# Moving rows of the big products at one place against the weights: padded input slots and SwiGLU tiles, rows 384 apart

## The chip, the cores and the metric

One core of one Trainium2 chip. The metric is the device time of one execution in microseconds. The kernel is one launch; everything below happens on that core: TensorE multiplies, VectorE, ScalarE and GpSimd work elementwise, and DMA queues issued from SyncE, ScalarE and GpSimd bring data between HBM and SBUF.

## The reference

One inference step of a hybrid trunk with two layers, on 128 context tokens and 256 latent tokens of width 1024 in float32. Each layer is a half-step SwiGLU block, a mixer with four head groups (mLSTM, global attention, windowed attention, Hyena convolution) that share an input and an output projection, and a second SwiGLU block. Before each stands an RMSNorm whose shift, scale and gate come from a conditioning vector.

```python
def swiglu(h, wg, wu, wd):
    return (jax.nn.silu(h @ wg) * (h @ wu)) @ wd

def trunk_layer(x, mod, p, mixer):
    h = rmsnorm(x, p['g_ff1']) * (1 + part(1)) + part(0)
    x = x + 0.5 * part(2) * swiglu(h, p['w1_gate'], p['w1_up'], p['w1_down'])
    h = rmsnorm(x, p['g_mix']) * (1 + part(4)) + part(3)
    y, ctx_state = mixer(h)
    x = x + part(5) * y
    h = rmsnorm(x, p['g_ff2']) * (1 + part(7)) + part(6)
    x = x + 0.5 * part(8) * swiglu(h, p['w2_gate'], p['w2_up'], p['w2_down'])
```

The hidden width of SwiGLU is 2816, the joint input projection has 2832 columns, the modulation `silu(c) @ w_ada + b_ada` has 9 x 1024 columns per layer.

## The kernel before

All 384 tokens are worked on together, with the model width on the partitions: `x` is eight blocks of 128 partitions by 384 columns. A big product is done in three parts (`prod3`, L241 to L244): weights and rows are each split into a high half of type float32r and the low rest, and high x high (L242), high weights x low rows (L243) and low weights x high rows (L244) are added up in PSUM. Each part is one matmul with a 128x128 weight block as the stationary operand and a row of 384 columns as the moving one, preceded by its own weight load.

Weights come from HBM in tiles of 4096 bytes a partition (`weights_load`), are split by ScalarE and VectorE into the pools `whi` and `wlo` (`weights_split`, L237 and L238), and live there in four buffers each. Right behind those pools in SBUF lies the pool `hx` with four input slots `w0` to `w3`, taken by the functions `wide` (eight rows of 386 columns) and `flat` (the same bytes as a staging buffer for the modulation weights and the first input). The slots are allocated in the order of first use: 2, 3, 0, 1. A `Norm` holds its un-normed, gained input in one pair of slots (`alloc_x`: the high half `xh`, the low half `xl`, with two extra columns for the shift) and the normed input in the other pair (`alloc_h`: `hh` and `hl`). Layer 0's first block and layer 1's last block have their normed rows in slots 2 and 3, the two blocks between them in slots 0 and 1. `ch` and `cl` are the mixer's concatenated output, written into a pair of slots and read by the output projection.

A SwiGLU block (`ffn`) runs gate and up for eleven pairs of hidden columns, then down for four pairs of output columns. The first pair of columns uses the gained rows of 386 columns; all later ones the normed rows of 384. The hidden activations are kept split in 22 tiles `ah` and 22 tiles `al` of 384 columns (`hid_tiles`), allocated behind the pools `sm` (small tiles) and `ht` (scratch). Beside gate, up and down in the first three blocks runs the modulation of later sublayers: VectorE multiplies and adds `w_ada` rows (L272) from the slots that hold no rows.

In the mixer, q and k of the mLSTM are products like the above; the token-major products (`tok_major`, L759 to L761) take the rows as the stationary operand and stream 512 weight columns. `gsml` holds `g_mlstm` on all partitions: GpSimd issues its load at the mixer's start (L746), and VectorE multiplies the output gate `so` with it (L873). The tile `dg` of the pool `sm` (one buffer, 128 x 3 x 128) is written in `rbcast` (L425) and read by the product behind it (L427). In `hyena_filters`, `coarse` splits `filt_w1` into two tiles of the pool `filt`.

The instructions of an engine run in their queue's order. A planner of the tile framework places most of them by readiness; stretches under `manual_schedule` keep the written order. A tile's next user waits until its last reader has ended.

Of the kernel before, what the change touches and what calls it, by code (L numbers as in the profile page):

```python
# [9 lines left out]
F32 = mybir.dt.float32  # L10
F32R = mybir.dt.float32r
# [6 lines left out]
P = 128  # L18
DM = 1024
KD = DM // P  # L20
NP_, NS = 128, 256
NT = NP_ + NS
DEPTH = 2
# [67 lines left out]
def trunk_kernel(ctx: ExitStack, tc: tile.TileContext, I: dict, C: dict, O: list):  # L91
    nc = tc.nc
# [7 lines left out]
    hx = ctx.enter_context(tc.tile_pool(name="hx", bufs=1))  # L100
    sm = ctx.enter_context(tc.tile_pool(name="sm", bufs=2))
# [4 lines left out]
    def mm(name):  # L106
        return pmm.tile([P, 512], F32, tag="mm", name=name)

    def small(name):
        return psm.tile([P, 512], F32, tag="sm", name=name)  # L110
# [4 lines left out]
    def cload(name, shape, src, pool=None, eng=None):  # L115
        t = (pool or const).tile(shape, F32, name=name)
        (eng or nc.gpsimd).dma_start(out=t, in_=src)
        return t

    XC = NT + 2

    def wide(i):
        return hx.tile([P, KD, XC], F32R, tag=f"w{i}", name=f"wide{i}")

    def flat(i, n):
        return hx.tile([P, KD * XC], F32, tag=f"w{i}", name=f"flat{i}")[:, :n]

    rows, ctile = {}, {}  # L130

# [22 lines left out]

    cols_c = columns("c", [("c", row128(I["c"]), 8, nc.sync), ("c_ctx", I["c_ctx"].rearrange("(k p) -> k p", p=P), 8, nc.scalar)])
    xst = flat(2, 3 * DM).rearrange("p (b d) -> p b d", b=3)
    for b in range(3):
        nc.sync.dma_start(out=xst[:, b, :], in_=I["x_prompt"][0] if b == 0 else I["x_sample"][0, (b - 1) * P:b * P, :])
# [57 lines left out]
    def weights(src, nk, ncol, name, paired=False):  # L216
        return weights_split(weights_load(src, nk, ncol, name, paired), nk, ncol, name)
# [23 lines left out]
    def prod3(out, lh, ll, rh, rl, start, stop):  # L241
        T.matmul(out, lhsT=lh, rhs=rh, start=start, stop=False)  # L242
        T.matmul(out, lhsT=lh, rhs=rl, start=False, stop=False)  # L243
        T.matmul(out, lhsT=ll, rhs=rh, start=False, stop=stop)  # L244

    def split(src, hi, lo):
        S.copy(hi, src)  # L247
        V.tensor_tensor(out=lo, in0=src, in1=hi.bitcast(F32), op=ALU.subtract)
# [72 lines left out]
    def stager(pair):  # L321
        turn = [0]

        def stage(n):
            turn[0] ^= 1
            return flat(2 * pair + turn[0], KD * n * P).rearrange("p (k f) -> p k f", k=KD)
        return stage
# [49 lines left out]
    class Norm:  # L377
# [16 lines left out]
        def alloc_x(self):  # L394
            self.xh, self.xl = wide(2 * self.pair), wide(2 * self.pair + 1)
# [22 lines left out]
        def shift_cols(self):  # L418
            b = mod[:, self.l, self.sh * KD:(self.sh + 1) * KD, :]
            split(b, self.xh[:, :, NT:XC], self.xl[:, :, NT:XC])  # L420

# [7 lines left out]
            S.copy(self.r, rb[:, :NT])  # L429

        def alloc_h(self):
            th, tl = wide(2 - 2 * self.pair), wide(3 - 2 * self.pair)
            self.hh = [th[:, k, :NT] for k in range(KD)]
            self.hl = [tl[:, k, :NT] for k in range(KD)]

        def apply(self):
            self.alloc_h()
# [32 lines left out]
    def ffn(l, wg, wu, wd, gate, name, nm, nxt, units, mid=None, last=None, pre=None):  # L470
        with pre["pools"] if pre else ExitStack() as pools:
            ht = pre["ht"] if pre else pools.enter_context(tc.tile_pool(name="ht" + name, bufs=2, reuse_waits="tile"))
            ah, al = [], []

            def hid_tiles(i, f0, f1):
                hid = pools.enter_context(tc.tile_pool(name=f"hid{i}{name}", bufs=1, reuse_waits="tile"))
                for f in range(f0, f1):
                    for q, ts in (("h", ah), ("l", al)):
                        ts.append(hid.tile([P, NT], F32R, name=f"a{q}{f}"))
# [10 lines left out]
            def gate_up(j, kc):  # L490
                if (j, kc) not in ahead:
                    ahead[j, kc] = {q: weights(w_ap[l][kc * P:(kc + KC) * P, j * CW:(j + 1) * CW], KC, CW, f"{q}{name}{j}_{kc}")
                                    for q, w_ap in (("g", wg), ("u", wu))}
                return ahead[j, kc]
# [3 lines left out]
            def join(p, m):  # L498
# [3 lines left out]
                for i, q in enumerate("gu"):  # L502
                    S.copy(bt[:, i, :], p[q][m][:, NT:XC])
                joined[m] = sg, su, bt

            for j in range(KF // 2):
                early = j == 0
                first = early and pre
                p = pre if first else {"g": [mm(f"pg{m}") for m in range(2)], "u": [mm(f"pu{m}") for m in range(2)]}
                for kc in range(0, KD, KC) if not first else ():  # L510
                    w = gate_up(j, kc)
# [13 lines left out]
                    for i, (k, m, q) in enumerate(order):  # L525
                        kk = kc + k
                        lh, ll = w[q][0][:, k, m * P:(m + 1) * P], w[q][1][:, k, m * P:(m + 1) * P]
                        if early:
                            prod3(p[q][m][:, :XC], lh, ll, nm.xh[:, kk, :], nm.xl[:, kk, :], kk == 0, kk == KD - 1)
                        else:  # L530
# [19 lines left out]
                for m in range(2):  # L550
                    f = 2 * j + m
# [19 lines left out]
            for cp in range(4):  # L571
                pd = [mm(f"pd{m}") for m in range(2)]
                for k0 in range(0, KF, KC):
                    nk = min(KC, KF - k0)
                    w = weights(wd[l][k0 * P:(k0 + nk) * P, cp * CW:(cp + 1) * CW], nk, CW, f"d{name}{cp}_{k0}")
# [27 lines left out]
    def hyena_filters(fp):  # L603
# [4 lines left out]
        w1 = fp.tile([34, DEPTH, 64], F32, name="fw1")  # L608
# [33 lines left out]
        cols_f(tc.keep_in_program_order)  # L642
        fr = col("filt_freq")

        def coarse(t, shape, magic, name):
            c = fp.tile(shape, F32, name=name + "c")
            f = fp.tile(shape, F32, name=name + "f")
            tc.keep_in_program_order(V.tensor_scalar(out=c, in0=t, scalar1=magic, scalar2=None, op0=ALU.add))
            V.tensor_scalar(out=c, in0=c, scalar1=magic, scalar2=None, op0=ALU.subtract)
            V.tensor_tensor(out=f, in0=t, in1=c, op=ALU.subtract)  # L650
            return c, f

        w1c, w1f = coarse(w1, [34, DEPTH, 64], 1.5 * 2.0 ** 16, "fw1")
        frc, frf = coarse(fr, [P, 1], 1.5 * 2.0 ** 17, "ffr")
        pA, pB = small("fpsA"), small("fpsB")
        for l in range(DEPTH):
# [78 lines left out]
    def mixer(l, K, nm, nxt, fill):  # L737
# [4 lines left out]
        mes = ExitStack()  # L742
        ml = mes.enter_context(tc.tile_pool(name=f"ml{l}", bufs=1, reuse_waits="tile"))
        nm.shift_cols()
        gsml = ml.tile([P, 256], F32, name="gsml")
        nc.gpsimd.dma_start(out=gsml, in_=I["g_mlstm"][l:l + 1].partition_broadcast(P).rearrange("p o d -> p (o d)"))  # L746
        cmask = cload(f"cmask{l}", [P, 512], C["cmask"], mx)
        rope = cload(f"rope{l}", [P, 2, 2, HD], C["rope"].rearrange("(b p) a d -> p b a d", p=P), mx)

        def tok_major(ps, c0, name):  # L750
            for kc in range(0, KD, 2):
                w = weights(win_l[kc * P:(kc + 2) * P, c0:c0 + 512], 2, 512, f"{name}{kc}")
                fill(6)
                fill.flush(99)
                for b in range(3):
                    tb = slice(b * P, (b + 1) * P)
                    for k in range(2):
                        kk = kc + k
                        T.matmul(ps[b], lhsT=hh[kk][:, tb], rhs=w[0][:, k, :], start=(kk == 0), stop=False)  # L759
                        T.matmul(ps[b], lhsT=hl[kk][:, tb], rhs=w[0][:, k, :], start=False, stop=False)  # L760
                        T.matmul(ps[b], lhsT=hh[kk][:, tb], rhs=w[1][:, k, :], start=False, stop=(kk == KD - 1))  # L761
# [20 lines left out]
        for i, c0 in enumerate((C_AQ, C_AK)):  # L782
            p = [mm(f"pqk{m}") for m in range(2)]
            for kc in range(0, KD, KC):
                w = weights(win_l[kc * P:(kc + KC) * P, c0:c0 + CW], KC, CW, f"aqk{l}{i}{kc}")
                if i == 0 and kc:
                    rr = nm.rstd()
                for k in range(KC) if kc and i == 0 else (None,):
                    for m in range(2):
                        for k_ in (range(KC) if k is None else (k,)):  # L790
                            kk = kc + k_
                            prod3(p[m][:, :XC], w[0][:, k_, m * P:(m + 1) * P], w[1][:, k_, m * P:(m + 1) * P], nm.xh[:, kk, :], nm.xl[:, kk, :], kk == 0, kk == KD - 1)
                if i == 0 and kc:
                    nm.rbcast(rr)
                    nm.apply()
            pq += p
        hh, hl = nm.hh, nm.hl
        ch, cl = (wide(2 * nm.pair + i)[:, :, :NT] for i in range(2))

        def qk_scaled():  # L800
            for i in range(4):
# [59 lines left out]
                S.copy(gt[:, i, :, d * 4:d * 4 + 4], prv[:, i, :, d * GB:d * GB + 4])  # L861
        at, emt, wi = gt[:, 0], gt[:, 1], gt[:, 2, 1:3]

        pvo = [mm(f"pvo{b}") for b in range(3)]
        tok_major(pvo, C_AV, f"avo{l}")
        va = ml.tile([P, 3, 4, HD + 1], F32, name="va")
# [11 lines left out]
        for d in range(2):  # L878
            for par in range(2):
# [3 lines left out]
                                    in_=I["state_mlstm_n"][0, l, d].rearrange("(hh par) (d o) -> par d hh o", par=2, o=1)[par],  # L883
# [27 lines left out]
        for h in range(4):  # L911
            c = h // 2
# [418 lines left out]
        with tc.manual_schedule(engines={nc.tensor.engine}):  # L1331
# [4 lines left out]
            for q in range(2):  # L1336
                p = [mm(f"pwo{m}") for m in range(4)]
                for i, k0 in enumerate((0, 2, 4, 6)):
                    w_src = I["w_out"][l][k0 * P:(k0 + 2) * P, q * 512:(q + 1) * 512]
                    w = weights(w_src, 2, 512, f"wo{l}{q}{k0}", paired=k0 in (2, 4))  # L1340
# [23 lines left out]
    def start(sp):  # L1364
# [86 lines left out]
        load_ada(1, 1)  # L1451
        load_ada(0, 1)
        residual_in(n0.acc, flat(3, 3 * DM).rearrange("p (b d) -> p b d", b=3))
        for s in range(2):
            S.copy(sc32[:, :, s], sc[:, :, s])
# [56 lines left out]
    with tc.tile_pool(name="start", bufs=1, reuse_waits="tile") as sp, tc.manual_schedule():  # L1512
        start(sp)
    fps = ExitStack()
    filters = hyena_filters(fps.enter_context(tc.tile_pool(name="filt", bufs=1, side="right", reuse_waits="tile")))
    next(filters)

# [25 lines left out]
    nm = n0  # L1543
# [3 lines left out]
    for l in range(DEPTH):  # L1547
        nx = Norm(f"m{l}", l, 3, 4, pair=nm.pair)
        ffn(l, I["w1_gate"], I["w1_up"], I["w1_down"], 2, f"a{l}", nm, nx, plan["a", l], between if l == 0 else None, pre=p0 if l == 0 else None)
        nm, nx = nx, Norm(f"b{l}", l, 6, 7, pair=1 - nx.pair)  # L1550
        mixer(l, K, nm, nx, Filler(plan["m", l], small_stage))
        nm = nx
        nx = Norm("a1", 1, 0, 1, pair=nm.pair) if l == 0 else Norm("fin", early=False, pair=nm.pair)
        ffn(l, I["w2_gate"], I["w2_up"], I["w2_down"], 8, f"b{l}", nm, nx, plan["b", l])
        nm = nx
# [4 lines left out]
    for b in range(3):  # L1560
        y = wst.tile([P, WCH], F32, tag="wst", name=f"y{b}")
        for q in range(2):
            p = small("pfin")
# [37 lines left out]
```

## Time and profile before

| | us |
|---|---|
| three runs | 1649.02, 1646.46, 1649.88 |
| median | 1649.02 |
| the profiled execution | 1645.32 |
| its span, from first to last instruction | 1643.5 |
| TensorE busy in it | 1592.4 (97%) |
| VectorE busy | 1233.9 (75%) |
| ScalarE busy | 775.3 (47%) |

The profiled execution is one execution of the same program, recorded by the hardware profiler; its span lacks what lies ahead of the first and behind the last instruction. A busy share is an average over stages. Matmuls are pipelined: one begins before the last has drained, so their durations overlap, and the time that a product costs is the distance between two starts.

### The profile page before, as it was taken

The page shows a single profiled execution, that of the slowest core. Times are in us where ns is not written, and L with a number is a line of the kernel's source. Part 1 is how long each engine was busy: PE and PEld are TensorE (multiplying, and loading weights), DVE is VectorE, ACT ScalarE, POOL GpSimd, SP SyncE. Part 2 cuts the span into 40 slices and gives each one's busy share as a digit, 9 for nine tenths or more (in the row PEclk, how much of TensorE's full clock was granted, in tenths as well). Part 3 has the DMA queues.
Part 4 walks back from the last instruction along what each step waited for, and adds up shares of the span by engine and source line. Part 5 has one row for each costly group of instructions (what it writes and reads, how often), then busy time and mean ns, then how long its engine had stood idle before and what let it go on. Part 6 is the DMA issues. An engine that isn't in the chain of part 4 may idle for free.

```text
span 1643.5 us, 24971 instructions
## 1 busy us (share of the span) xinstructions
PE 1592.4 (97%) x9169; PEld 1497.7 (91%) x9169; DVE 1233.9 (75%) x2402; ACT 775.3 (47%) x1815; POOL 248.7 (15%) x334
## 2 busy tenths in 40 slices
PE   7899999999989999999999999999998999999997
PEld 4799999997867999999999999999776799999997
DVE  4899998996856699986999986697795567434333
ACT  4544444367454554443546444345835556333321
POOL 2122322241120001221220211113103000000000
PEclk9999999999999999999999999999999999999999
DMA  9667757853332367757667764765333234444341
GB/s 329 199 204 233 220 176 230 254 152 110 93 90 65 103 214 237 231 177 232 210 180 222 230 202 148 247 200 152 101 101 81 65 103 124 122 127 129 116 135 58
DMA packets 235855, 271.22 MB, mean 165 GB/s; under 512 B 14367, under 2 KB 220415, under 8 KB 235732
## 3 DMA queue, kind: packets, MB, share of 16 engines
q1 hardware_dynamic: 223232, 248.67, 49.0%
q0 software_dynamic: 9472, 20.30, 5.0%
q8 instruction: 72, 1.18, 0.3%
q10 hardware_dynamic: 3028, 0.64, 0.2%
q14 instruction: 51, 0.42, 0.1%
HBM read 257.62 MB, written 3.57 MB: 159 GB/s over the span
## 4 chain that ended last, share of the span: by engine, by line
PE 80%; DVE 12%; ACT 4%; issue 2%; DMA 1%; ACTq 0%; DVEq 0%
PE pg L242 7%; PE pg L243 7%; PE pg L244 7%; PE pu L244 7%; PE pu L243 7%; PE pu L242 7%; PE pd L244 5%; PE pd L243 5%; PE pd L242 5%; DVE adacc L272 4%; PE pwo L242 1%; PE pwo L243 1%; PE pwo L244 1%; PE pa L760 1%; PE pdu L242 1%
## 5 line engine op out<-in xcount | busy, mean ns | idle before, releaser
L272 DVE SCALAR_TENSOR_TENSOR adacc<-flat,sc,adacc 128x384 f32<-128x384 f32 (+1 forms) x602 | 353.5, 639 | 0.0
L296 POOL TENSOR_TENSOR adfold<-adacc,adfold 64x384 f32<-64x384 f32 (+1 forms) x86 | 119.5, 1390 | 138.3 <-DMA adfold<-adacc 135.8
L242 PE MATMUL pd<-ah,hi_da 128*128 128x384 f32 x352 | 120.1, 341 | 0.0
L244 PE MATMUL pd<-ah,lo_da 128*128 128x384 f32 x352 | 119.3, 339 | 0.8 <-DVE lo_da L238 0.8
L244 PE MATMUL pd<-ah,lo_db 128*128 128x384 f32 x352 | 119.3, 339 | 0.6 <-DVE lo_db L238 0.6
L243 PE MATMUL pg<-wide,hi_gb 128*128 128x384 f32 (+1 forms) x352 | 119.6, 340 | 0.2
L242 PE MATMUL pd<-ah,hi_db 128*128 128x384 f32 x352 | 119.7, 340 | 0.0
L242 PE MATMUL pg<-wide,hi_gb 128*128 128x384 f32 (+1 forms) x352 | 119.6, 341 | 0.0
L243 PE MATMUL pd<-al,hi_db 128*128 128x384 f32 x352 | 119.2, 339 | 0.0
L243 PE MATMUL pd<-al,hi_da 128*128 128x384 f32 x352 | 119.1, 338 | 0.0
L244 PE MATMUL pg<-wide,lo_gb 128*128 128x384 f32 (+1 forms) x352 | 119.0, 338 | 0.0
L243 PE MATMUL pu<-wide,hi_ub 128*128 128x384 f32 (+1 forms) x352 | 118.8, 338 | 0.0
L244 PE MATMUL pu<-wide,lo_ub 128*128 128x384 f32 (+1 forms) x352 | 118.4, 338 | 0.0
L242 PE MATMUL pu<-wide,hi_ub 128*128 128x384 f32 (+1 forms) x352 | 118.2, 337 | 0.0
L247 ACT CAST ah<-sg 128x384 fp32r<-128x384 f32 x88 | 45.0, 512 | 151.3 <-DVE sg L561 149.7
L292 POOL DMA_DIRECT2D adfold<-adacc x43 | 23.3, 542 | 599.1 <-DVE adacc L272 356.1
L242 PE MATMUL pg<-wide,hi_ga 128*128 128x384 f32 (+1 forms) x328 | 112.4, 343 | 0.0
L244 PE MATMUL pg<-wide,lo_ga 128*128 128x384 f32 (+1 forms) x328 | 111.2, 339 | 0.0
L243 PE MATMUL pg<-wide,hi_ga 128*128 128x384 f32 (+1 forms) x328 | 111.1, 339 | 0.0
L242 PE MATMUL pu<-wide,hi_ua 128*128 128x384 f32 (+1 forms) x328 | 110.5, 337 | 0.4 <-DVE sg L561 0.4
L244 PE MATMUL pu<-wide,lo_ua 128*128 128x384 f32 (+1 forms) x328 | 110.8, 338 | 0.0
L243 PE MATMUL pu<-wide,hi_ua 128*128 128x384 f32 (+1 forms) x328 | 110.7, 337 | 0.0
(496 smaller groups left out, 4294.1 us busy)
## 6 DMA issues: line engine op xcount, KB each, us to landing
flat<-in_w_ada_dram SPq DMA_DIRECT2D x42, 1536.0 KB, 7.9
st_gb<-in_w_gate_dram SPq DMA_DIRECT2D x44, 512.0 KB, 3.8
st_ub<-in_w_up_dram SPq DMA_DIRECT2D x44, 512.0 KB, 4.7
st_ga<-in_w_gate_dram SPq DMA_DIRECT2D x41, 512.0 KB, 4.0
st_ua<-in_w_up_dram SPq DMA_DIRECT2D x41, 512.0 KB, 5.1
st_da<-in_w_down_dram SPq DMA_DIRECT2D x40, 512.0 KB, 4.7
st_db<-in_w_down_dram SPq DMA_DIRECT2D x40, 512.0 KB, 3.8
wst<-in_w_ada_dram SPq DMA_DIRECT2D x8, 1024.0 KB, 11.5
```

The source lines that it names most:

```text
L242: T.matmul(out, lhsT=lh, rhs=rh, start=start, stop=False)
L243: T.matmul(out, lhsT=lh, rhs=rl, start=False, stop=False)
L244: T.matmul(out, lhsT=ll, rhs=rh, start=False, stop=stop)
L247: S.copy(hi, src)
L272: last_step[0] = V.scalar_tensor_tensor(out=acc[:, s, :n * P], in0=w[:, k, :], scalar=sc[:, k, s:s + 1], in1=acc[:, s, :n * P], op0=ALU.mu ...
L292: nc.gpsimd.dma_start(out=fold[0:64, :c], in_=acc[64:128, 0, :c])
L296: G.tensor_tensor(out=fold[h, :c], in0=acc[h, s, :c], in1=fold[h, :c], op=ALU.add)
L760: T.matmul(ps[b], lhsT=hl[kk][:, tb], rhs=w[0][:, k, :], start=False, stop=False)
```

## The change

The pool `hx` gets a pad tile of 16 floats (64 bytes a partition) ahead of the slots. A slot becomes 3136 floats (12544 bytes, 49 x 256) instead of 8 x 386. The gained rows (`wide`) still lie 386 apart in it; normed rows and the mixer's output (`rows_of`) now lie 384 apart. The pool `ht` gets a pad tile of 40 floats (160 bytes), behind which the SwiGLU tiles lie. The pads are never read or written. Two users have no tiles of their own any more: `gsml`, and the two parts of `filt_w1`, now lie in the tile `dg`. The load of `gsml` moves from the mixer's start to the place behind the copies of the gate rows.

```diff
     XC = NT + 2
+    SLOT = 3136
+    hx.tile([P, 16], F32, name="hxpad")
+
+    def slot(i, dt, name):
+        return hx.tile([P, SLOT], dt, tag=f"w{i}", name=f"{name}{i}")
 
     def wide(i):
-        return hx.tile([P, KD, XC], F32R, tag=f"w{i}", name=f"wide{i}")
+        return slot(i, F32R, "wide")[:, :KD * XC].rearrange("p (k t) -> p k t", k=KD)
+
+    def rows_of(i):
+        return slot(i, F32R, "wide")[:, :KD * NT].rearrange("p (k t) -> p k t", k=KD)
 
     def flat(i, n):
-        return hx.tile([P, KD * XC], F32, tag=f"w{i}", name=f"flat{i}")[:, :n]
+        return slot(i, F32, "flat")[:, :n]
...
         def alloc_h(self):
-            th, tl = wide(2 - 2 * self.pair), wide(3 - 2 * self.pair)
-            self.hh = [th[:, k, :NT] for k in range(KD)]
-            self.hl = [tl[:, k, :NT] for k in range(KD)]
+            th, tl = rows_of(2 - 2 * self.pair), rows_of(3 - 2 * self.pair)
+            self.hh = [th[:, k, :] for k in range(KD)]
+            self.hl = [tl[:, k, :] for k in range(KD)]
...
             ah, al = [], []
+            ht.tile([P, 40], F32, name="htpad", bufs=1)
...
-        def coarse(t, shape, magic, name):
-            c = fp.tile(shape, F32, name=name + "c")
-            f = fp.tile(shape, F32, name=name + "f")
+        def coarse(t, shape, magic, name, cf=None):
+            c, f = cf or (fp.tile(shape, F32, name=name + q) for q in "cf")
...
-        w1c, w1f = coarse(w1, [34, DEPTH, 64], 1.5 * 2.0 ** 16, "fw1")
+        w1s = sm.tile([P, 3, P], F32, tag="dg", bufs=1, name="fw1s")
+        w1c, w1f = coarse(w1, None, 1.5 * 2.0 ** 16, "fw1", [w1s[:34, i, :].rearrange("p (l f) -> p l f", l=DEPTH) for i in range(2)])
...
-        gsml = ml.tile([P, 256], F32, name="gsml")
-        nc.gpsimd.dma_start(out=gsml, in_=I["g_mlstm"][l:l + 1].partition_broadcast(P).rearrange("p o d -> p (o d)"))
...
-        ch, cl = (wide(2 * nm.pair + i)[:, :, :NT] for i in range(2))
+        ch, cl = (rows_of(2 * nm.pair + i) for i in range(2))
...
+        gsml = sm.tile([P, 3, P], F32, tag="dg", bufs=1, name="gsml").rearrange("p b t -> p (b t)")[:, :256]
+        nc.gpsimd.dma_start(out=gsml, in_=I["g_mlstm"][l:l + 1].partition_broadcast(P).rearrange("p o d -> p (o d)"))
         pvo = [mm(f"pvo{b}") for b in range(3)]
```

## Rows read from the trace of the kernel before

**Rows 1.** The page: span, busy time of the engines, and the chain that ended last.

```profile
span 1643.5 us, 24971 instructions
...
PE 1592.4 (97%) x9169; PEld 1497.7 (91%) x9169; DVE 1233.9 (75%) x2402; ACT 775.3 (47%) x1815; POOL 248.7 (15%) x334
...
PE 80%; DVE 12%; ACT 4%; issue 2%; DMA 1%; ACTq 0%; DVEq 0%
```

**Rows 2.** Stage windows, TensorE alone: stretch, length, busy (count), clock, DMA share, GB/s.

```profile
283.53:300.12 16.59, 16.59 (x95) 1.00 0.70 217
...
1537.12:1630.21 93.09, 93.09 (x528) 1.00 0.31 99
151.71:168.16 16.45, 16.45 (x95) 1.00 0.73 219
1370.67:1537.11 166.44, 166.44 (x951) 1.00 0.43 125
585.59:625.79 40.20, 40.20 (x230) 1.00 0.73 233
```

**Rows 3.** Stage windows, all engines: PE, PEld, DVE, ACT, POOL; two down stages.

```profile
255.00:351.00 96.00, 95.25 (x546) 94.72 (x545) 92.32 (x156) 43.10 (x116) 24.58 (x28) 1.00 0.76 229
...
1537.00:1630.00 93.00, 93.00 (x528) 93.00 (x527) 31.63 (x43) 23.63 (x28) 0.57 (x1) 1.00 0.31 99
```

**Rows 4.** Timeline at 1600 us, last block's down stage: start, duration, engine, line.

```profile
1600.19 0.34 PE L242 MATMUL pd<-ah,hi_db 128*128 128x384 f32 x1
1600.19 0.19 PEld L243 LDWEIGHTS pd<-al,hi_db 128*128 128x128 f32 x1
```

**Rows 5.** Groups of instructions by line and shape, TensorE: count, busy us, mean ns.

```profile
L242 PE MATMUL pd<-ah,hi_da 128*128 128x384 f32 x352 | 120.1, 341 | 0.0
...
L242 PE MATMUL pg<-wide,hi_gb 128*128 128x384 f32 x320 | 108.5, 340 | 0.0
...
L242 PE MATMUL pg<-wide,hi_ga 128*128 128x384 f32 x312 | 106.9, 343 | 0.0
...
L242 PE MATMUL pwo<-wide,hi_wo 128*128 128x384 f32 x128 | 44.8, 350 | 0.0
```

**Rows 6.** Timeline, single products of gate and up in first and last block.

```profile
70.62 0.34 PE L242 MATMUL pg<-wide,hi_pre10g 128*128 128x384 f32 x1
70.80 0.34 PE L243 MATMUL pg<-wide,hi_pre10g 128*128 128x384 f32 x1
...
1526.59 0.34 PE L242 MATMUL pu<-wide,hi_ub 128*128 128x384 f32 x1
1526.77 0.34 PE L243 MATMUL pu<-wide,hi_ub 128*128 128x384 f32 x1
...
68.53 0.33 PE L242 MATMUL pg<-wide,hi_pre10g 128*128 128x384 f32 x1
...
1527.64 0.33 PE L242 MATMUL pu<-wide,hi_ub 128*128 128x384 f32 x1
...
71.84 0.34 PE L243 MATMUL pg<-wide,hi_pre10g 128*128 128x384 f32 x1
...
1527.28 0.34 PE L243 MATMUL pu<-wide,hi_ub 128*128 128x384 f32 x1
```

**Rows 7.** Instructions by tile (`gsml`, `dg`) and a row of GpSimd's timeline.

```profile
L746 POOL DMA_DIRECT2D gsml<-in_g_mlstm_dram x2: 573/573/573, 352.4 to 1134.9; - x2
L873 DVE TENSOR_TENSOR so<-so,gsml x2: 950/952/954, 401.2 to 1183.9; 128x768 f32<-128x768 f32 x2
...
DMA to landing us min/median/max: 4.0/4.7/5.4
...
L427 PEld LDWEIGHTS rbm<-dg,ones x4: 186/188/189, 362.3 to 1145.8; 128*128 128x128 f32 x4
...
391.94 1.00 POOL L849 DMA_DIRECT2D out_dram<-gE  x2
```

## The prediction

> **What bounds the kernel now.** I read the page's busy table first: TensorE is busy 97% of a span of 1643.5 us, VectorE 75% [rows 1]. The chain that ended last runs 80% over TensorE and 12% over VectorE [rows 1]. So a product that takes less time shortens the span, as long as nothing else is close behind. The question is what sets the time of one product, and for that the stage windows are the view. They hold runs in which one 384-column product follows the next without a gap; the count has one product more than there are intervals, because one is still running when the window opens. In the down products the interval is 16.59/94 = 176.5 ns in the first block and 93.09/527 = 176.6 in the last [rows 2]. In gate and up it is 16.45/94 = 175.0 in the first block and 166.44/950 = 175.2 in the last, but 40.20/229 = 175.5 in the second [rows 2]. The granted clock is 1.00 in all of them, so the array runs at 2.4 GHz, where 384 columns are 160 ns. Some 15 ns of each product are something else.
>
> That something is neither a wait nor a loaded neighbour: the down products keep their 176.5 to 176.6 while VectorE is busy 92.32 of 96 us and 31.63 of 93, and the DMA share is 0.76 and 0.31 [rows 2, 3]. It does differ with the place of the operands. Each weight load begins with the product before it [rows 4], so the array reads one product's moving row and the next one's weights together. I call "distance" the number of bytes that a moving row starts past the weights, modulo 256. It comes out of the code: a weight tile has 4096 bytes and its 128-column blocks start 512 bytes apart, so all weights have one phase. An input slot has 8 x 386 x 4 = 12352 bytes, 64 more than a multiple of 256, and its rows are 1544 apart, 8 more than a multiple. The slots stand in the order 2, 3, 0, 1 right behind the weights, at 0, 64, 128 and 192. So the first and last block read rows at (8k, 64 + 8k) for high and low half, the two between at (128 + 8k, 192 + 8k), and the SwiGLU tiles, 1536 bytes each, are all at 96, by the sizes of what lies between. Three placements, three paces: 175.1, 175.5 and 176.6. Placement is worth something; between stages it is 1.5 ns in 176.
>
> **The change, part by part.** *Rows to distance 64.* It moves 6288 products that run without gaps: 6 x 352 = 2112 down, 6 x 312 and 6 x 320 = 3792 gate and up, 3 x 128 = 384 output (one line of each kind stands in [rows 5]). Of gate and up 1872 belong to first and last block and 1920 to the two between. Hyena's and the gates' columns stand in gaps of other work and are not counted. What a product takes at a constant 64 no stage shows, so I bound it from single rows. Row k = 0 of the low half in first and last block is at 64: the 90 intervals behind such products have a mean of 174.7 ns (first at 70.80, last at 1526.77 [rows 6]). But a start that is late lengthens one interval and shortens the next, so the sum over the three products of one k is safer: at k = 0 it is 526.1 ns (67 triples, from 70.62 to 1526.59 [rows 6]). The products at distance 0 in it have 176.0 each by their own intervals, which leaves 526.1 - 352.0 = 174.1 for the one at 64. Below that: the best k, with the triple at 16 and 80, has a median of 172.0 a product (75 triples, from 68.53 to 1527.64 [rows 6]). Above: the next low-half row, at 72, has 178.0 (93 intervals, from 71.84 to 1527.28 [rows 6]). I take 174.0, because the rows at 64 itself lie nearest, and of their two readings the one that is a sum.
>
> At 174.0: down 2112 x 2.6 = 5.5 us; gate and up 1872 x 1.1 = 2.1 and 1920 x 1.5 = 2.9; output, taken at the pace of the block that follows it, 384 x 1.5 = 0.6. Sum 11.1 us. At 172.0 it is 9.7 + 5.8 + 6.7 + 1.3 = 23.5 us; at 178.0 a loss of 3.0 + 5.4 + 4.8 + 1.0 = 14.2. Today's weighted mean is 175.8, so 1 ns is 6.3 us, and 175.8 is the point at which the sign turns.
>
> Does all of it reach the end? Behind TensorE stands VectorE, with 92.32 of 96 us in the first block's down stage and 31.63 of 93 in the last [rows 3]; the second block has filler work like the first, so I take it as equal. At 174.0 such a stage of 528 products shrinks by 1.4 us and VectorE still fits; at 172.0 it would shrink to some 93.6, still above. Below that two of the four down stages stop gaining.
>
> *The fused-column products* (386 wide, 544 of them) keep slots with rows of 386; their distances go from four classes plus 8k to 64 + 8k throughout. I count 0, and with the 3 ns by which single rows lie either side of the mean, 1.6 us either way. *The token-major products* hold the rows as weights and stream 512 columns; their distance becomes a constant 192. 432 of them by the same 3 ns are 1.3 us either way, taken at 0.
>
> *g_mlstm's load* moves from the mixer's start into the tile `dg`, behind the last read of it, the broadcast product near 362.3 and 1145.8 [rows 7]. Its 0.57 us on GpSimd's queue moves past the eight state loads and, if nothing brings it forward, past the two row stores and the two final-state stores; the last of these end at 392.94 [rows 7]. Then it has issued by 393.5, lands 4.0 to 5.4 us later, by 398.9, and is read at 401.2 [rows 7]. The cover is 2.3 us. Without it VectorE would wait in its multiply, and behind that the inter-chunk products and all of the score work; a load that slipped by 5 us would cost 2.7 us a layer. The score-row loads behind it start 0.57 us later, so at worst twice 0.57 us are lost there. Counted 0, with 6.5 us as the far end. *The split of filt_w1* into the same `dg` is the same three VectorE instructions; `dg` lies free from the first block's broadcast to the mixer's. Counted 0, for the same reason: nobody holds the tile. The two padding tiles have no instructions.
>
> The profiled execution took 1645.3 us (the span and 1.8 around it): 1645.3 - 11.1 = 1634.2. The median of the three runs lies 3.7 us above it: 1637.9.
>
> **A rule that speaks against it.** The down stages show 176.6 ns where 160 are streamed at clock 1.00, and 175.0 to 175.5 at other distances [rows 2]. The Trainium skill (TensorE: Matmul & The Clock Gate, "Step-by-step: what each phase is for") holds that the array has two independent SBUF read ports and that loading the next weights does not steal read bandwidth from the running product. By that, distance could not matter and the time would stay at 1649. The stage windows disagree, by 1.5 ns a product. The rule leads to rival B below.
>
> **The rivals.**
> A, a deeper cut: with every product at one distance the two reads settle into a rhythm that the mixed rows never reach. For: single rows span 172.0 to 178.0, so 6 ns are in play. Against: the rows at 64 show no such drop. At 172.0: 1625.5. At 169, with two down stages held at VectorE's 92.3 us: 6288 x 6.8 = 42.8, less 2 x (92.3 - 528 x 0.169 = 3.1), 36.6 us, 1612.
> B, only the order of costs changes: any placement averages to what the mixed rows average to, within 0.5 ns of 175.8. For: the two input placements differ by 0.4 ns only once they are averaged over k. Result 1649, give or take 3.3. That the tiles don't land at 64, because the padding falls elsewhere, ends here too.
> C, slower: products at one distance repeat one meeting of the two reads instead of averaging over eight, as those at 96 do today (176.6, the slowest stage). For: the next row, at 72, has 178.0 [rows 6]. Against: 64 itself has 174.1 to 174.7. At 178.0: 1663. It decides as soon as the common pace is above 175.8; the down products lose little, gate and up most.
>
> **How the numbers follow.** Forecast (173 to 175.2 ns, 1632 to 1645): 0.42. A: 0.20. B: 0.19. C: 0.19. About 0.2%, 3.3 us, is what a measurement of this kernel can tell from no change. Faster by more: forecast and A, 0.62; within: 0.19; slower: 0.19. The range may leave out 0.2: it takes the forecast and B, A down to 169 ns (1612), and C up to a pace of 176.9 (1656), which also holds the forecast with the far ends of the uncounted parts.
>
> **What would show it.** In the four down stages the interval must leave 176.6, and gate and up of all blocks must come to one pace, the same as down and output, because all have distance 64. 174.0 is the forecast, 172 or less is A, 175.3 to 176.3 is B, more is C. Different paces of down and gate/up would say that bits above 256 count too, and that my measure is wrong. The weight loads must still begin with the product before, and clock 1.00 must hold. g_mlstm's multiply must stay near 401 less what was gained before it, with no idle time of VectorE ahead of it. The forecast falls if single rows at 64 between neighbours at 0 say nothing about a steady 64; that is its weakest step.

## The result, and the profile after

| | before | after |
|---|---|---|
| median, us | 1648.69 | 1670.86 |
| lowest to highest | 1646.46 to 1649.88 | 1669.31 to 1673.47 |
| ratio, 95% interval | | 1.0153, 1.0136 to 1.0170 |
| the profiled execution's span | 1643.5 | 1668.0 |

The change makes the kernel 1.5% slower, 22 us. The forecast was 1637.9 us, with 1612 to 1656 as its range: wrong, and on the other side. The page of after, span, busy time and the chain that ended last, answers to [rows 1]:

```profile
span 1668.0 us, 24967 instructions
...
PE 1591.6 (95%) x9169; PEld 1493.3 (90%) x9169; DVE 1230.6 (74%) x2402; ACT 774.9 (46%) x1815; POOL 256.0 (15%) x334
...
PE 78%; DVE 12%; ACT 5%; DMA 2%; issue 2%; ACTq 0%; SPq 0%; DVEq 0%
```

TensorE is busy about as long as before (1591.6 against 1592.4), in a span that is 24.5 us longer: time in which TensorE does nothing was added. That the two sums agree is chance: without the added time the same products are busy 1573.0 us (first experiment below), and part of what the faster paces saved is spent again at a lower clock, as shown further down. The stage windows, TensorE alone, have the paces at clock 1.00 (columns as in [rows 2]; the number of intervals is counted by the starts inside a stretch):

```profile
794.04:810.34 16.30, 16.30 (x96) 1.00 0.70 214
1562.96:1654.31 91.35, 91.35 (x529) 1.00 0.31 101
148.91:165.20 16.29, 16.29 (x95) 1.00 0.72 221
1397.08:1562.79 165.71, 165.71 (x958) 1.00 0.43 126
597.72:638.63 40.91, 40.91 (x238) 1.00 0.74 229
```

Down takes 16.30/94 = 173.4 ns in the second block and 91.35/527 = 173.3 in the last, where [rows 2] have 176.5 in the first and 176.6 in the last. Gate and up take 16.29/94 = 173.3, 165.71/956 = 173.3 and 40.91/236 = 173.3, where they had 175.0, 175.2 and 175.5. All stages have come to one pace, as the prediction asked for, and it is 0.7 ns below the 174.0 that it took. This part of the change works.

The loss stands between the blocks. In the waits of TensorE (waited for, us in total, times, longest) these rows are on top, where before only one wait of 0.4 us for `accm` was found:

```profile
PE stb L419 <- DVE accb L399: 12.3, 2, 6.1
PE stm L419 <- DVE accm L399: 8.6, 2, 4.6
...
PE sta L419 <- DVE acca L399: 4.5, 1, 4.5
...
PE pqk L251 <- ACT wide L256: 2.3, 2, 1.2
```

I took the start of the last product of a block and the start of the next one's first product from the timeline, for all five boundaries:

| boundary | before | after |
|---|---|---|
| first down to the mixer's q and k | 351.20 to 351.38 | 348.28 to 354.69 |
| output to the second block | 564.6 to 564.8 | 569.05 to 576.82 |
| second down to layer 1 | 850.9 to 851.0 | 861.53 to 868.91 |
| third down to q and k | 1135.3 to 1135.5 | 1149.87 to 1157.15 |
| output to the last block | 1349.6 to 1349.8 | 1368.97 to 1376.74 |

After, that is 6.41 + 7.77 + 7.38 + 7.28 + 7.77 = 36.6 us, before five times 0.2: 35.6 us were added. The span grew by 24.5; the 11.1 between are what the faster products gave back, less what the lower clock behind the gaps took. The timeline of the first boundary, all engines (start, duration, engine, line, and in brackets the idle time before and what ended it), shows what TensorE waits for:

```profile
348.28 0.34 PE L253 MATMUL pd<-ah,lo_da 128*128 128x384 f32 x1
348.42 1.38 DVE L467 SCALAR_TENSOR_TENSOR xt<-pd,mod,xt 128x128 f32<-128x128 f32 x4
...
352.54 0.99 PE L419 MATMUL stm<-ones,accm 128*128 128x1 f32 x6 [3.92 <-DVE accm L399]
...
353.85 0.55 DVE L257 TENSOR_TENSOR wide<-nt,wide 128x384 fp32r<-128x384 f32 x1
...
354.44 0.20 ACT L256 CAST wide<-mod 128x16 fp32r<-128x16 f32 x1 [1.23 <-DVE wide L257]
...
354.69 0.69 PE L251 MATMUL pqk<-wide,hi_aqk 128*128 128x386 f32 x1 [1.16 <-ACT wide L256]
```

Read it from below. The first product waits for a cast that writes 16 values a partition, the high half of the two shift columns of all eight rows (`shift_cols`). The cast waits for the low half of the last gained row. That row waits for the last residual (L467), which needs the last down product. Before, the same cast had long been done:

```profile
233.90 0.20 ACT L247 CAST wide<-mod 128x16 fp32r<-128x16 f32 x1 [5.43 <-DVE adacc L272]
...
355.22 0.55 DVE L248 TENSOR_TENSOR wide<-nt,wide 128x384 fp32r<-128x384 f32 x1
```

At 233.90 it ran 117 us ahead of the product that reads it (351.38). The last gained rows were no earlier than they are now: their low halves start at 355.22 and behind it, while TensorE works on the first ones. What is new is that the first product must wait for the last row. The rms sum (`stm`, L419), which stood behind the first products, has moved ahead of them in TensorE's order, and so the view of the waits puts most of the gap down to it. The same holds at all five boundaries: the casts start at 233.9, 528.9, 717.0, 983.3 and 1314.0 before, 36 to 152 us ahead of the products that read them, and at 354.4, 576.0, 868.7, 1156.9 and 1375.9 after, each less than 1 us ahead.

A gap costs more than itself, in the stretch behind it. The first row is after, the second is before over as long a time from the same product on (columns as above, the last three being granted clock, DMA share and GB/s):

```profile
354.69:359.89 5.20, 4.96 (x14) 0.50 0.09 25
...
351.38:356.58 5.20, 5.20 (x33) 1.00 0.94 257
```

The granted clock is 0.50 there, the lower of the two levels 1.2 and 2.4 GHz, and fewer than half as many products run as before. TensorE had stood idle for 5 of the 6 us ahead of that stretch. The same is found behind the other four gaps, for 3.0 to 4.9 us each at 0.50, where before has 1.00.

The rows of the moved load, read by tile, answer to [rows 7]:

```profile
L873 POOL DMA_DIRECT2D gsml<-in_g_mlstm_dram x2: 583/583/583, 367.0 to 1169.1; - x2
L883 DVE TENSOR_TENSOR so<-so,gsml x2: 949/950/950, 403.9 to 1206.0; 128x768 f32<-128x768 f32 x2
...
DMA to landing us min/median/max: 3.4/3.4/3.4
```

It is issued at 367.0, lands at 370.4 and is read at 403.9. Nothing waits for it.

### The profile page after: what moved, and what is told of

It is laid out like the page before. It is cut to its first block, busy times and chain, and to the rows that moved or that the text cites. A ratio compares the mean times of both kernels' runs of the same rounds, so it can differ in the third digit from the quotient of the medians.

```text
span 1668.0 us, 24967 instructions
## 1 busy us (share of the span) xinstructions
PE 1591.6 (95%) x9169; PEld 1493.3 (90%) x9169; DVE 1230.6 (74%) x2402; ACT 774.9 (46%) x1815; POOL 256.0 (15%) x334
## 4 chain that ended last, share of the span: by engine, by line
PE 78%; DVE 12%; ACT 5%; DMA 2%; issue 2%; ACTq 0%; SPq 0%; DVEq 0%
PE pg L251 7%; PE pg L252 7%; PE pu L251 7%; PE pg L253 7%; PE pu L252 7%; PE pu L253 7%; DVE adacc L281 4%; PE pd L251 4%; PE pd L252 4%; PE pd L253 4%; PE pa L768 1%; PE pa L769 1%; PE pa L767 1%; PE pwo L251 1%; PE pwo L252 1%
## 5 line engine op out<-in xcount | busy, mean ns | idle before, releaser
L305 POOL TENSOR_TENSOR adfold<-adacc,adfold 64x384 f32<-64x384 f32 (+1 forms) x86 | 126.2, 1467 | 140.9 <-DMA adfold<-adacc 138.6
```

The source lines that it names most:

```text
L305: G.tensor_tensor(out=fold[h, :c], in0=acc[h, s, :c], in1=fold[h, :c], op=ALU.add)
```

## The experiments

Theory 1: the declaration does it. `wide` was a tile of its own shape and is now a stretch cut out of a longer tile (`[:, :KD * XC]`) and folded into rows. With that view, the writes of the shift columns are ordered behind all writes of gained rows, although no byte is shared. Rival 2: the new addresses, the moved load or the shared tile `dg` do it. Rival 3: a faster down stage exposes the last residual, which would come under any declaration.

**The declaration undone, all addresses kept.** Every product stands at 64 as in the changed kernel.

```diff
     def wide(i):
-        return slot(i, F32R, "wide")[:, :KD * XC].rearrange("p (k t) -> p k t", k=KD)
+        return hx.tile([P, KD, XC], F32R, tag=f"w{i}", name=f"wide{i}")
```

> The changed kernel, with one declaration undone: a gained input is again a tile of its own shape, 128 x 8 x 386, in the same slot at the same addresses, and no longer a stretch cut out of the slot of 3136 floats. Every distance stays at 64. Theory 1 (the cut view makes the writes of the shift columns wait for all gained rows, and the next block's first product waits for them): the shift columns are written 100 us ahead again, the five gaps of 6.4 to 7.8 us at the block boundaries (36.6 us) shrink to the 0.2 us they had before, and the time is 1671 - 35.6 = 1635 us, between 1633 and 1639; the pace of the down products stays at 173.3 ns. Rival 2 (the gaps come from the new addresses, the moved load or the shared tile dg): nothing changes, 1671 us. Rival 3 (the gaps are the last residual of a block, which a faster down stage now exposes): the wait moves to another instruction, gaps of 4 us and more remain, 1655 us or above.

Measured: 1630.63 us, before on the same chip 1645.98; ratio 0.9914 (0.9889 to 0.9938). The boundary, TensorE's timeline, and ScalarE's cast:

```profile
346.25 0.34 PE L253 MATMUL pd<-ah,lo_da 128*128 128x384 f32 x1
346.43 0.34 PE L251 MATMUL pqk<-wide,hi_aqk 128*128 128x386 f32 x1
...
229.69 0.21 ACT L256 CAST wide<-mod 128x16 fp32r<-128x16 f32 x1 [5.43 <-DVE adacc L281]
```

The five gaps are gone (0.18 us here), the cast is 117 us early again, and the last down stage keeps its 91.3 us. Rivals 2 and 3 fall: addresses, load, `dg` and paces are those of the changed kernel. The time is 4 us below what I expected, and below the range that I gave. I had left out what the clock loses behind a gap, and this chip ran the kernel before 2.7 us faster; how the 4 us divide between the two was not measured.

**The declaration alone, with the old distances.** The pads are out, the rows 386 apart, and a slot 64 floats longer, so that every phase is that of before; the load and `dg` stay changed.

```diff
-    SLOT = 3136
-    hx.tile([P, 16], F32, name="hxpad")
+    SLOT = KD * XC + 64
...
-        return slot(i, F32R, "wide")[:, :KD * NT].rearrange("p (k t) -> p k t", k=KD)
+        return wide(i)[:, :, :NT]
...
-            ht.tile([P, 40], F32, name="htpad", bufs=1)
```

> The changed kernel with the old distances (input rows at 0, 64, 128 and 192 plus 8k, SwiGLU tiles at 96): rows 386 apart, slots 64 floats longer, no pads. The cut view, the moved load and the shared dg stay. Theory 1: the shift columns are written behind the last gained row, five gaps of 6 to 8 us stand at the block boundaries, the paces are those of before (176.6 in down, 175.0 to 175.5 in gate and up), and the time is 1649 + 35 = 1684 us, between 1679 and 1688. Rival 2, as far as it lays the gaps to the new addresses: no gaps, 1649 us. Rival 3 (a faster down stage exposes the residual): no gaps, because down is not faster here, 1649 us.

Measured: 1685.57 us, ratio 1.0247 (1.0220 to 1.0273). One of the five boundaries, TensorE's timeline, and ScalarE's cast:

```profile
868.50 0.33 PE L252 MATMUL pd<-ah,lo_db 128*128 128x384 f32 x1
873.49 1.44 PE L418 MATMUL sta<-ones,acca 128*128 128x1 f32 x6 [4.65 <-DVE acca L398]
876.09 0.69 PE L250 MATMUL pg<-wide,hi_ga 128*128 128x386 f32 x1 [1.16 <-ACT wide L255]
...
875.83 0.20 ACT L255 CAST wide<-mod 128x16 fp32r<-128x16 f32 x1 [2.51 <-DVE wide L256]
```

All five gaps are there, 6.7 to 7.7 us from start to start, at the paces of before, and the cast waits for the last gained row again. The cut view costs 40 us whether the products are fast or slow: 1.0247 here, and 1.0153 / 0.9914 = 1.0241 between the changed kernel and the one with the declaration undone.

**The load and the two users of `dg` alone**, on the kernel before.

```diff
-        gsml = ml.tile([P, 256], F32, name="gsml")
+        gsml = sm.tile([P, 3, P], F32, tag="dg", bufs=1, name="gsml").rearrange("p b t -> p (b t)")[:, :256]
...
+        w1s = sm.tile([P, 3, P], F32, tag="dg", bufs=1, name="fw1s")
```

> The kernel before with two parts of the change alone: g_mlstm's load moved into the tile dg behind the copies of the gate rows, and the two parts of filt_w1 in dg. Slots, views and distances are those of before. The prediction's step (both are covered): within 3.3 us of 1649, g_mlstm's multiply near 401 us with no idle time of VectorE ahead of it. Its far end: the load slips and VectorE waits, up to 6.5 us more, 1655. Rival 2, as far as it lays the gaps to the moved load or to dg: five gaps of some 7 us, 1684 us.

Measured: 1643.34 us, ratio 0.9994 (0.9978 to 1.0010), no gaps. The load is issued at 365.7 and its reader starts at 402.72, behind a matrix of the scores and without idle time of its own. The zero of the prediction holds.

**The order of writes turned round, the cut view kept.** `shift_cols` is called where the gained input is allocated, ahead of its rows, instead of at the start of the next block.

```diff
             if k == 0 and self.early:
                 self.alloc_x()
+                self.shift_cols()
...
-            if not pre:
-                nm.shift_cols()
...
-        nm.shift_cols()
```

> The changed kernel with the cut view kept, but the writes of the shift columns put ahead of the block's gained rows in the written order, where the gained input is allocated, instead of behind them. Theory 1 (an order of writes that the cut view enforces): the shift columns no longer have anything to wait for, no gaps, 1635 us, between 1633 and 1640. A variant of theory 1 (not the order of writes holds, but each product that reads a row of a cut view waits for every write into it): the gaps stay at 6 to 8 us, 1671 us, because the last gained row is still late. Rival 3: gaps stay, 1655 us or above.

Measured: 1630.13 us, ratio 0.9906 (0.9880 to 0.9931). The cast runs early again, and the boundary has no gap:

```profile
230.78 0.21 ACT L256 CAST wide<-mod 128x16 fp32r<-128x16 f32 x1 [5.43 <-DVE adacc L281]
...
347.45 0.34 PE L253 MATMUL pd<-ah,lo_da 128*128 128x384 f32 x1
347.62 0.34 PE L251 MATMUL pqk<-wide,hi_aqk 128*128 128x386 f32 x1
```

The time is 3 us below the range that I gave, as in the first experiment. So the view does not make readers wait for every write into the tile; it enforces the written order of writes. Here, with the early thing written first, the cut view costs nothing: 0.9906 against 0.9914 for the tile of its own shape.

**Other distances.** Four kernels with the declaration undone, one execution of each. In the first, normed rows stand at 0 and the SwiGLU tiles at another distance in each block; in the second, rows at 128.

```diff
-    hx.tile([P, 16], F32, name="hxpad")
...
-            ht.tile([P, 40], F32, name="htpad", bufs=1)
+            pad = {'a0': 40, 'b0': 48, 'a1': 8, 'b1': 0}[name]
+            if pad:
+                ht.tile([P, pad], F32, name="htpad", bufs=1)
```

> The changed kernel with gained inputs as tiles of their own shape (no gaps at the block boundaries), other distances: all normed rows at 0, and the SwiGLU tiles at 0 in the first block, 32 in the second, 128 in the third, 96 in the last. Each down stage is read by its own pace. Theory of a phase (the pace depends on the distance modulo 256 and on nothing else): the last block's down products take the 176.6 ns that 96 had before, gate and up at 0 take the same time as the first block's down products at 0, and 0, 32 and 128 lie between 173 and 179 ns each. Rival (64 is fast because rows and tiles lie at the same distance or because the rows are 384 apart): down at 96 takes 173.3 ns too. Theory of two ports (the distance does not count): 173.3 ns in all.

Measured: 1632.98 us. Stage windows, TensorE alone: down at 0, 32, 128 and 96, then gate and up at 0.

```profile
281.47:297.81 16.34, 16.34 (x95) 1.00 0.70 213
776.66:792.95 16.29, 16.29 (x95) 1.00 0.73 228
1031.75:1048.46 16.71, 16.71 (x96) 1.00 0.97 314
1524.79:1617.89 93.10, 93.10 (x528) 1.00 0.30 99
1360.06:1524.62 164.56, 164.56 (x951) 1.00 0.41 127
```

The second has a pad of 32 floats ahead of the slots and `{'a0': 48, 'b0': 56, 'a1': 0, 'b1': 24}`.

> As before it, with all normed rows at 128 and the SwiGLU tiles at 160 in the first block, 192 in the second, 224 in the third, 64 in the last. Theory of a phase: the last block's down products take 173.3 ns; gate and up at 128 take the same as the down products at 128 in the run beside this one; 160, 192 and 224 lie between 173 and 179 ns, and if one of them lies below 173.3 there is something left to gain. Theory of two ports: 173.3 ns in all.

Measured: 1642.87 us. Down at 160, 192, 224 and 64, then gate and up at 128:

```profile
284.87:301.17 16.30, 16.30 (x96) 1.00 0.68 223
783.15:799.44 16.29, 16.29 (x95) 1.00 0.70 231
1110.79:1131.26 20.47, 20.47 (x120) 1.00 0.49 143
1536.46:1627.80 91.34, 91.34 (x528) 1.00 0.31 101
1369.26:1536.28 167.02, 167.02 (x950) 1.00 0.40 125
```

Interval by distance, length over intervals:

| distance | 0 | 32 | 64 | 96 | 128 | 160 | 192 | 224 |
|---|---|---|---|---|---|---|---|---|
| ns | 173.8, 173.4 | 173.3 | 173.3 | 176.7 | 175.9, 176.0 | 173.4 | 173.3 | 173.5 |

96 gives the pace of before in another kernel and another block, and where a distance was taken both by down and by gate and up (0 and 128), the two agree within 0.4 ns.

In the third kernel the normed rows are 386 apart (`return wide(i)[:, :, :NT]` in `rows_of`), so that they run from 64 to 120 in steps of 8; the SwiGLU tiles stay at 64.

> The changed kernel with gained inputs as tiles of their own shape, normed rows 386 instead of 384 apart in all four slots: their distances are 64 + 8k instead of 64, the SwiGLU tiles stay at 64. If the distance of each product counts by itself, as the single rows of the trace before say (174.1 ns at 64, 178.0 at 72), gate and up go to a mean above 174.5 ns while down stays at 173.3, and the time is 6 us or more above that with rows 384 apart. Rival (only the slot's start counts): gate and up stay at 173.6 ns, 1630 us.

Measured: 1643.61 us. Gate and up, and down, of the last block:

```profile
1369.48:1536.64 167.16, 167.16 (x950) 1.00 0.40 125
1536.82:1628.16 91.34, 91.34 (x528) 1.00 0.32 101
```

Gate and up are back at 167.16/949 = 176.1 ns, down stays at 173.3. The rival falls: it is the row pitch, not only the start of the slot, that has to fit. That each product counts by itself is not shown, and single intervals speak against it. In the trace before, products at distance 0 between other rows take 176.0 ns (the prediction's reading), and those at 192 in the two middle blocks some 177.5 (the 72 intervals behind row k = 0 of the low half). In steady stretches 0 takes 173.4 to 173.8 and 192 takes 173.3.

In all of these the weights lie at one phase, so that a row's distance and its own address modulo 256 cannot be told apart. The fourth kernel moves the weights.

```diff
+    whi.tile([P, 16], F32, name="wpad", bufs=1)
-    hx.tile([P, 16], F32, name="hxpad")
+    hx.tile([P, 24], F32, name="hxpad")
...
-            ht.tile([P, 40], F32, name="htpad", bufs=1)
+            ht.tile([P, {'a0': 32, 'b0': 32, 'a1': 48, 'b1': 24}[name]], F32, name="htpad", bufs=1)
```

> The changed kernel with gained inputs as tiles of their own shape, and the weights themselves moved by 64 bytes (a pad of 16 floats in whi; wlo follows). So far all weights lay at one phase, so that the distance of a row and its own address modulo 256 could not be told apart. Here the normed rows stand at distance 96 from the weights, but at the own address that belonged to distance 160 in the earlier runs; the SwiGLU tiles of the third block at distance 128 and the address that belonged to 192, those of the last block at distance 32 and the address that belonged to 96, those of the first two at distance 64 and the address that belonged to 128. If the distance sets the pace: gate and up 176.7 ns, down 176.0 in the third block and 173.3 in the last. If the row's own address sets it: gate and up 173.4, down 173.3 in the third block and 176.7 in the last, and the weight loads have no part in it.

Measured: 1642.36 us. Gate and up of the last block, down of the third and of the last:

```profile
1367.45:1535.11 167.66, 167.66 (x951) 1.00 0.40 125
1038.84:1055.56 16.72, 16.72 (x97) 1.00 0.98 314
1535.29:1626.63 91.34, 91.34 (x528) 1.00 0.31 101
```

167.66/949 = 176.7 ns at distance 96, 16.72/95 = 176.0 at 128, 91.34/527 = 173.3 at 32: all three go by the distance and against the address. So the weights are half of the matter. A product pays for where its row lies against the weights that are loaded beside it. Rival B falls. The Trainium skill (TensorE: Matmul & The Clock Gate, "Step-by-step: what each phase is for") says that loading the next weights takes no read bandwidth from the running product. For these float32r products the runs disagree: at clock 1.00 on both sides the same product takes 173.3 or 176.7 ns by its distance to the weights. By what mechanism the two reads meet is not shown.

**Each half of the placement alone.** The kernel before with only the SwiGLU tiles at 64, by one line (`ht.tile([P, 56], F32, name="htpad", bufs=1)`):

> The kernel before with one line: a pad of 56 floats in ht, so that the SwiGLU tiles alone move from 96 to 64. Input slots, rows and views are those of before. The down products go from 176.6 to 173.3 ns. If the stages shrink with their products, each of the four down stages loses 528 x 3.3 = 1.7 us, 7.0 us in all. If VectorE holds the first two (it is busy 92 of 96 us in them), they lose 0.3 to 0.5 and the last two 1.7 to 1.8, 4.3 us in all: 0.9974 of the time before. No gaps at the block boundaries, and gate and up stay at 175.0 to 175.5 ns.

Measured: 1641.42 us, before on this chip 1643.19; ratio 0.9986 (0.9973 to 1.0000). Two down stages, all engines (PE, PEld, DVE, ACT, POOL), answer to [rows 3]:

```profile
259.80:355.50 95.70, 94.20 (x547) 92.95 (x546) 92.00 (x156) 43.33 (x117) 25.45 (x28) 1.00 0.74 230
1538.40:1629.70 91.30, 91.30 (x528) 91.30 (x527) 31.63 (x43) 23.59 (x28) 0.57 (x1) 1.00 0.31 101
```

The last stage shrinks by 1.8 us, the first by 0.4, with VectorE still at 92.00: the second case of the expectation, 4.3 us. The time alone does not show it: the ratio of 0.9986 is 2.3 us, and its interval runs from those 4.3 us to no change. And the kernel with the declaration undone and `htpad` at 48 floats, only the rows at 64:

> The changed kernel with gained inputs as tiles of their own shape, and a pad of 48 instead of 40 floats in ht: the SwiGLU tiles stand at 96 as before, the normed rows alone at 64. Down stays at 176.6 ns, gate and up come to 173.3 in stretches without gaps, output to 173.3. By the stage lengths of the kernel with all at 64 this is 9.6 us of gate and up and 0.9 of output, 10.5 us: 0.9936 of the time before. If the two parts don't add up to the 15.4 us that they had together, one of them frees time that the other needs.

Measured: 1636.37 us, ratio 0.9953 (0.9934 to 0.9972). The stage lengths are the expected ones: 187.9, 187.3 and 185.3 us for the last three gate and up stages (190.0, 189.4 and 187.2 before), 36.8 for output. The two ratios multiply to 0.9939, both parts together gave 0.9914; with intervals of 0.002 and more on each that is no proof of a surplus, and whether there is one stays open.

## Why the prediction was wrong, point by point

- **What bounds the kernel, and that placement is worth something:** right. TensorE's pace sets the stages, and the pace went where the distance went.
- **The pace at 64, its "weakest step":** the number is near, 174.0 against 173.3 at a steady 64, but the way to it was luck. The same reading of single rows gives 176.0 for distance 0, where a steady stretch has 173.4 to 173.8, and 177.5 for 192, where it has 173.3. Single rows between others at other distances do not tell a steady pace, and the prediction could not know that its reading at 64 would be one of the good ones. The bound above it, 178.0 for the row at 72, is not reached by the rows from 64 to 120 together: 176.1.
- **Two readings that are a little off:** the stretches in the first two blocks begin and end up to 10 ns beside a start. Counted from start to start, down in the first block takes 176.7 ns, gate and up 175.2 there and 175.6 in the second. And there are 576 products of 386 columns, not 544. Neither changes the forecast.
- **The sum of 11.1 us:** with the declaration undone the gain is 0.0086 of the time, 14.2 us (10 to 18), which on the median of before, 1648.69, makes 1634.5, within the forecast's 1632 to 1645. So without the gaps the forecast of 1637.9 would have stood 3 us beside the time. The terms: output 37.3 and 37.2 to twice 36.8, 0.9 us (0.6 forecast). The last three gate and up stages 2.1, 2.1 and 1.9 us, and the first, 936 products at 175.2 - 173.3 = 1.9 ns, 1.8: 7.9 in all (5.0 forecast). Down 0.5, 0.3, 1.7 and 1.8, 4.3 us (5.5 forecast).
- **"VectorE still fits" in the first two down stages:** wrong by a little. The stages don't end at VectorE's 92.1 us of work, they shrink from 96.1 to 95.6 and from 95.9 to 95.6. At 173.3 ns TensorE's 528 products need 91.5. Part of the rest is other products (548 matmuls run in the window of such a stage, 528 in the last), part waits for weights that VectorE splits (`lo_da` and `lo_db`, 0.8 and 0.6 us in TensorE's waits before, 1.6 each with the declaration undone). VectorE, busy 96% of such a stage, held it in part although the sum of its busy time would have fitted: the prediction compared the sums and not the moments at which TensorE needs what VectorE makes.
- **gsml, fw1 and the pads at zero:** right (0.9994). That the load slips to 393 was too careful: it was brought forward to 367.0.
- **The step that failed: the slots.** The prediction treated the new slots as a change of addresses and of nothing else. It gives each moved load its queue and each pad its instructions, but no term to the declaration of `wide`, and none of its rivals has one: A, B and C are about paces. The declaration is worth 40 us, nearly three times the gain. The rows for it stood in the trace before: a cast at 233.90 whose place in the written order is at 351, and gained rows at 355.22 that end behind the first product of their block. Both say that the order of these writes was free, and what it costs if it is not: the time from the end of a block to its last gained row, some 7 us, five times.
- **The range:** it took in the paces from 169 to 176.9, and the time fell out of it at the top by 15 us, because its bounds were those of the costs that the sum named.

How the framework arrives at the wait (whether it sees a cut and folded view as one closed stretch) is not shown. Shown is that the wait comes with the cut view at old and new addresses, goes with a tile of its own shape at the same addresses, and goes when the shift columns are written first. Whether the cut or the folding does it, no run tells apart.

## What to carry to other kernels

A change of a tile's declaration can be a change of the dependences: before pricing the addresses, list the instructions that write into the tile, and look in the trace for those that run far ahead of their written place, because these are what a coarser view takes away. Pad so that every moving row keeps one good distance to its weights, pitch included, but leave the tile in its own shape; that version takes 1630.6 us where before takes 1646.0, and beats both kernels. Where a view has to be cut, write what is ready early before what comes late. Read a pace from a steady stretch, not from single products between others.

## What the runs showed of the hardware

- Where all rows lie at one distance, the time of a 384-column float32r product goes by the distance modulo 256 between its row and the weights loaded beside it, also when the weights are moved. The lowest is 173.3 ns at clock 1.00, the same in down, gate and up, and output (with the declaration undone, 23.40 us for 135 intervals of output), reached at 32, 64, 160 and 192 bytes within 0.1 ns, within 0.2 ns at 224, and nearly at 0. 96 and 128 cost 3.3 and 2.7 ns more. 64 is not special; before stood at the slowest of the eight for down. There is no faster one among the multiples of 32. The figures at 0, 160, 192 and 224 rest on one execution each. A row's own interval between rows at other distances can lie 2 to 4 ns beside its steady pace (0 and 192).
- Behind each of the five pauses of TensorE (6.4 to 7.8 us from start to start) the granted clock is 0.50 for 3.0 to 5.2 us of products, where before, without the pause, has 1.00 at the same products.
